# Rope on VectorE, the turns of q and k between blocks of the next projection, aligned tiles and earlier reloads of u in a hybrid S5 and attention layer

## The chip, the cores and the metric

The kernel runs on one core of a Trainium2 chip as one program. The metric is the device time in microseconds of one execution, as the median of several; a profiled execution gives the trace from which all rows below come. The engines are PE (TensorE, matmuls and transposes), ACT (ScalarE), DVE (VectorE), POOL (GpSimd) and SP (SyncE, which issues nearly all DMAs from one queue in order).

## The reference

One decoder layer, 512 positions, width 1024, one batch, float32. Cut to what matters:

```python
h = rms_norm(x, norm_w)
u_s, z_s, q, k, v, z_a, r_s, r_a = split(h @ w_in)
y_s = s5_branch(u_s, ...)                      # diagonal complex state space, GLU
y_s = (y_s * silu(z_s)) @ w_ssm_out
q, k = rms_norm(q, q_norm_w), rms_norm(k, k_norm_w)     # per head of 64
q, k = apply_partial_rope(q, pos), apply_partial_rope(k, pos)   # first 16 of 64
y_a = dilated_attention(q, k, v)               # 3 groups: window/dilation 128/1, 512/4, 2048/16
y_a = (y_a * silu(z_a)) @ w_attn_out
m = sigmoid(r_s) * y_s + sigmoid(r_a) * y_a
out = x + m @ w_o
```

There are three dilation groups (g = 0, 1, 2) of eight heads of 64 each.

## The kernel before, in words

**Projections in three products.** Each float32 operand is split into a rounded part (hi) and a rest (lo), and `mm3` (L130) makes three matmuls for each tile of 128 of the contraction: hi hi, hi lo, lo hi. A weight section of 512 KB is loaded by SP into `w_raw` (two buffers, `load_w`, L193), rounded by ACT into `w_hi` (L116) and subtracted by DVE into `w_lo` (L118), three buffers each. `plan` lists the sections in order, and `get_w` (L187) hands out the next one and starts loads two ahead. A unit (`cm_unit`, L203) is 24 matmuls of 512 columns into one bank of PSUM (`pj`).

**The order of the program.** The order in which the code names the work is only a priority. A planner places each engine's instructions by that priority among what it expects to be ready, and each engine then runs its list strictly in order. `queued()` (L69) adds a condition: PE instructions inside its block come after the PE instruction traced last.

**The u stage.** h is made and transposed (hT). Eight units `u_unit(j)` (L289) project u; each copies its bank out (uT, ACT) and stores it to a scratch in DRAM (`ud`, SP, L295), from which `load_u` (L271) reads it back in another layout: pieces of 256 bytes, into parts of `sza` for j = 0 to 3, each of which waits until the store has landed. In between, DVE makes the state-space coefficients, `w_unit` (L297) transposes them (wps, W) and `x_unit` (L313) multiplies them with the reloaded u (xps). The first three units are computed together; in the code their reloads follow `u_unit(3)` (L475 to L479).

**The middle.** Gates, the scan on DVE, the state-space output, its GLU and output projection. The change does not touch it.

**Attention, in four pairs of heads (hp).** Each pair takes two wide granules and a unit. A wide granule (`wide_granule`, L829) has four quarters kq of weights and, in each, four blocks r of 128 positions with six matmuls each: four pj banks are filled at once, and all of them are complete only in the last quarter. The first (`qk_first`, L896) gives q and k of groups 0 and 1, the second (`qk_second`, L908) q and k of group 2 and the values V of groups 1 and 2, and the unit `v0_unit` (L596) V of group 0. `qk_norm` (L846) makes the sums of squares, an inverse root by iteration, the scaling of `qraw` (DVE, L858), and then rope on POOL (L864 to L869): for each group, two products and an addition over 16 of 64 columns, four instructions. `qk_turn` (L871) transposes a group of normed q and k on PE (qtp), a = 0 for q and a = 1 for k, and ACT and DVE write hi and lo into `qkp`.

`scores` (L933) makes the scores (sps) and the softmax factors in `Pt`, which DVE scales last (L997). `values` (L1000) transposes `Pt` (ptp), copies each transposed bank to `ptb` (ACT for the first head of the pair, L1039, DVE for the second, L1041) and multiplies it with V (ot).

The banks of PSUM are dealt in turn: four for pj, three (4, 5, 6) for transposes and scores, taken in the order of the code, and the eighth for ot. V, Pt and the two qraw tiles have one buffer each.

In the loop over pairs (L1103 to L1122), while the softmax of pair hp is under way, the granules of pair hp + 1 run. The second granule calls `mid(kq)` ahead of a quarter: the turn of group 0 ahead of quarter 1, of group 1 ahead of quarter 2 (inside `queued()`), and `values(hp)` ahead of quarter 3. Then follow `v0_unit`, the turn of group 2 and the transposes of V. The last pair has no granules beside it, only units of the gate `ra`.

**Addresses.** Tiles of a pool lie one after another. In the built program of before, hT_hi and every large tile after it start 192 bytes past a multiple of 512.

Of the kernel before, what the change touches and what calls it, by code (L numbers as in the profile page):

```python
# [2 lines left out]

# [1 line left out]

# [47 lines left out]
def tile_hybrid_block(ctx: ExitStack, tc: tile.TileContext, x, positions, norm_w, w_in, lam_re, lam_im,  # L53
# [54 lines left out]
    def pj_tile():  # L108
        return ps_tile("p", "pj")
# [90 lines left out]
        split(hi, lo, raw, lo_eng=lo_w[0])  # L200
        return hi, lo

    def cm_unit(rh, rl, kts=KT):  # L203
        hi, lo = get_w()
        ps = pj_tile()
        for k in range(kts):
            mm3(ps, hi[:, k], lo[:, k], rh[:, k], rl[:, k], k == 0, k == kts - 1)
        return ps
# [5 lines left out]
    act.dma_start(nw8, norm_w[0].rearrange("(k p) -> k p", p=P))  # L214
    nwc = cst.tile([P, KT], F32, name="nwc")
    wcol = cst.tile([P, NG, 2], F32, name="wcol")
    hT_hi = cst.tile([P, KT, S], F32R, name="hT_hi")
    hT_lo = cst.tile([P, KT, S], F32R, name="hT_lo")
    nps = bank("nps")
# [51 lines left out]
    def load_u(j, Uj=None):  # L271
        if Uj is None:
            Uj = t2k("Uj")
        sp.dma_start(Uj, ud[j].rearrange("q g s c -> s q g c"))
        return Uj.rearrange("p (g c) -> p g c", g=8)
# [13 lines left out]
    def u_unit(j, ps=None):  # L289
        if ps is None:  # L290
            ps = cm_unit(hT_hi, hT_lo)
        uT = t2k("uT")

        act.copy(uT.rearrange("p (h r i j) -> p r j i h", h=2, r=4, i=NI), ps.rearrange("p (r j i h) -> p r j i h", r=4, h=2, i=NI))
        sp.dma_start(ud[j].rearrange("q g s c -> g q (s c)"), uT)  # L295
# [35 lines left out]
                mm3(ps[:, t], hi[:, k], lo[:, k], hT_hi[:, k, t], hT_lo[:, k, t], k == 0, k == KT - 1)  # L331
    for j in range(3):
        u_unit(j, first[j][1])
    lr = scr([G, N])
    li = scr([G, N])
    dt = scr([G, 1])
# [137 lines left out]

    for j in range(3, 8):  # L475
        u_unit(j)
        for i in {3: (0, 1, 2), 4: (3,)}.get(j, ()):
            early[i] = load_u(i, sza[:, i])
        wx(*((), (), (0,), (1,), (2, 3))[j - 3])  # L479


# [111 lines left out]
                            hi[:, k], lo[:, k], kh == 0 and k == 0 and rr == 0, kh == 1 and k == 3)  # L593
        return pss

    def v0_unit(hp, V):  # L596
        ps = cm_unit(hT_hi, hT_lo)
        vt = t2k("vt")
        act.copy(vt.rearrange("p (b r j) -> p r b j", r=4, b=4), ps.rearrange("p (r b j) -> p r b j", r=4, b=4))

        def finish():
            pt = bank("vtp")
            for b in range(NB):
                pe.transpose(pt[:, b * P:(b + 1) * P], vt[:, b * P:(b + 1) * P], ident)
            act.copy(V[:, 0].rearrange("p b c -> p (b c)"), pt)
        return finish
# [219 lines left out]
    if "gT" in dbg:  # L826
        sp.dma_start(dbg["gT"], gT_hi.bitcast(F32).rearrange("p k s -> p (k s)"))

    def wide_granule(th, tl, mid=None):  # L829

        pss = [pj_tile() for _ in range(NB)]
        for kq in range(4):
            if mid:
                mid(kq)
            hi, lo = get_w()
            for r in range(NB):
                for k in range(2):
                    kk = 2 * kq + k
                    mm3(pss[r], th[:, kk, r * P:(r + 1) * P], tl[:, kk, r * P:(r + 1) * P], hi[:, k], lo[:, k],
                        kk == 0, kk == KT - 1)  # L840
        return pss

    def new_raw(i):
# [2 lines left out]
    def qk_norm(gs, raws, sq):  # L846

        n = 4 * len(gs)
        v = sml.tile([P, 32], F32, name="qv", bufs=1)[:, 0:NB * n]
        rstd = sml.tile([P, 32], F32, name="qrstd", bufs=1)[:, 0:NB * n]  # L850
        qa = sml.tile([P, 32], F32, name="qa", bufs=1)[:, 0:NB * n]
        qb = sml.tile([P, 32], F32, name="qb", bufs=1)[:, 0:NB * n]
        dve.tensor_scalar(v.rearrange("p (r h) -> p r h", r=NB), sq, 1.0 / HD, EPS, op0=ALU.mult, op1=ALU.add)
        rsqrt(rstd, v, [P, NB * n], qa, qb)
        rs = rstd.rearrange("p (r h) -> p r h", r=NB)
        for i, (g, raw) in enumerate(zip(gs, raws)):
            rv = raw.rearrange("p r (h d) -> p r h d", h=4)
            dve.tensor_tensor(rv, rv, rs[:, :, 4 * i:4 * i + 4].unsqueeze(3).broadcast_to([P, NB, 4, HD]), op=ALU.mult)  # L858
            t1 = sml.tile([P, NB * 2, 2, 16], F32, name="rt1", bufs=1)
            t2 = sml.tile([P, NB * 2, 2, 16], F32, name="rt2", bufs=1)  # L860
            rh = raw.rearrange("p r (a h d) -> p (r a) h d", a=2, h=2)
            cv = tC[:, g].rearrange("p r a d -> p (r a) d").unsqueeze(2)
            sv = tS[:, g].rearrange("p r a d -> p (r a) d").unsqueeze(2)
            pool.tensor_tensor(t1, rh[:, :, :, 0:16], cv.broadcast_to([P, NB * 2, 2, 16]), op=ALU.mult)  # L864
            pool.tensor_tensor(t2[:, :, :, 0:8], rh[:, :, :, 8:16],
                               sv[:, :, :, 0:8].broadcast_to([P, NB * 2, 2, 8]), op=ALU.mult)
            pool.tensor_tensor(t2[:, :, :, 8:16], rh[:, :, :, 0:8],
                               sv[:, :, :, 8:16].broadcast_to([P, NB * 2, 2, 8]), op=ALU.mult)
            pool.tensor_tensor(rh[:, :, :, 0:16], t1, t2, op=ALU.add)  # L869

    def qk_turn(g, raw, QT, KA, KB):  # L871
        for a in range(2):
            ps = bank("qtp")
            pn = ps.rearrange("p (b r j) -> p r b j", r=4, b=4)
            for r in range(NB):
                o = pn[:, r] if g == 0 else ps[:, r * P:(r + 1) * P]
                pe.transpose(o, raw[:, r, a * P:(a + 1) * P], ident)
            if a == 0 or g == 0:
                parts = [(slice(0, P), QT[0][:, g], QT[1][:, g]) if a == 0 else (slice(0, P), KA[0], KA[1])]
            else:  # L880
                parts = [(slice(64 * h, 64 * h + 64), KB[0][64 * h:64 * h + 64, g - 1, h],
                          KB[1][64 * h:64 * h + 64, g - 1, h]) for h in range(2)]
            for sl, hi, lo in parts:
                w = wcol[sl, g, a:a + 1]
                act.activation(hi, ps[sl], AF.Copy, scale=w)  # L885
                dve.scalar_tensor_tensor(lo, ps[sl], w, hi.bitcast(F32), op0=ALU.mult, op1=ALU.subtract)  # L886
# [18 lines left out]
        qk_norm((0, 1), raws, sq)  # L905
        return raws

    def qk_second(hp, mid=None):  # L908

        pss = wide_granule(hT_hi, hT_lo, mid)  # L910
        raw = new_raw(0)
        V = new_v()
        sq = sml.tile([P, NB, 8], F32, name="ssq")[:, :, 0:4]
        for r in range(NB):
            act.copy(raw[:, r], pss[r][:, 0:256])
            squares(sq[:, r], pss[r][:, 0:256])
            act.copy(V[:, 1:3, r], pss[r][:, 256:512].rearrange("p (g c) -> p g c", g=2))  # L917
        qk_norm((2,), [raw], sq)
        return raw, V
# [80 lines left out]
    def values(hp, Pt, V):  # L1000
# [23 lines left out]
        for kind in range(2):  # L1024
            for bb in range(2):
                pts = []
                k0 = 1 if kind == 0 and bb == 0 else 0
                for h in range(2):
                    ps = bank("ptp")
                    for i in range(2):  # L1030
                        for k in range(2):
                            if 2 * i + k < k0:
                                continue
                            pe.transpose(ps[:, (2 * i + k) * P:(2 * i + k + 1) * P],
                                         Pt[:, h, kind, 2 * bb + i, k * P:(k + 1) * P], ident)
                    pt = PT[n % 4]
                    n += 1
                    if h == 0:
                        act.copy(pt[:, k0 * P:], ps[:, k0 * P:])  # L1039
# [63 lines left out]
    for hp in range(NP):  # L1103
        Pt = scores(hp, *QK)
        if hp < NP - 1:
            raws = qk_first()

            def mid(kq):
                if kq == 1:
                    qk_turn(0, raws[0], *QK)  # L1110
                if kq == 2:
                    with queued():
                        qk_turn(1, raws[1], *QK)
                if kq == 3:
                    values(hp, Pt, V)

            raw, V_next = qk_second(hp + 1, mid)
            V = V_next
            finv = v0_unit(hp + 1, V)
            qk_turn(2, raw, *QK)  # L1120
            finv()
        else:  # L1122
            for c in range(2):
                rals[c] = gate_tile()
                sp.dma_start(rals[c], rad[c])
            for c in range(n_ra + 1, KT - 2):
                ra_unit(c)
            values(hp, Pt, V)
            for c in range(KT - 2, KT):
                ra_unit(c)  # L1130
# [60 lines left out]
```

## Time and profile before

| what | value |
|---|---|
| median of 3 runs | 720.77 us (719.61 to 723.12) |
| the profiled execution's own time | 722.95 us |
| its span in the trace | 721.2 us |
| PE, PE weight loads | 689.3 us (96%), 571.6 us (79%) |
| DVE | 460.8 us (64%) |
| ACT | 314.8 us (44%) |
| POOL | 179.8 us (25%) |
| DMA, mean | 114 GB/s |

How to read it: busy times are of the whole span. PE's matmuls are pipelined and their ends are modelled, so a busy PE need not be at its peak, and a short stall can hide in a modelled end. A row of the waits gives who waited, for whom, the time in all, how often, and the longest. A row of the chain or the timeline starts with its time from the span's start and its length in us. A row of the groups gives, behind the bar, busy us, the mean ns of one, and the idle time of the engine just before, with who ended it.

### The profile page before, as it was taken

What the parts mean: (1) busy time and instruction counts of PE and PEld (TensorE: products, weight loads), DVE (VectorE), ACT (ScalarE), POOL (GpSimd) and SP (SyncE); (2) the same over time, 40 slices, a digit from 0 to 9 for tenths busy, and PEclk for the clock granted to TensorE, in tenths of its full rate; (3) what the DMA queues carried; (4) which work ended last, traced back from release to release, by engine and by line L of the source; (5) the groups of instructions that cost most, each with busy time, mean ns of one, the idle gap of its engine ahead of it and who ended that gap; (6) DMA issues with size and microseconds to landing.
All of it is one profiled execution on the core that took longest, in us unless ns stands there. A gap on an engine that the chain in (4) does not pass through costs nothing.

```text
span 721.2 us, 12599 instructions
## 1 busy us (share of the span) xinstructions
PE 689.3 (96%) x4789; PEld 571.6 (79%) x4789; DVE 460.8 (64%) x928; ACT 314.8 (44%) x631; POOL 179.8 (25%) x330
## 2 busy tenths in 40 slices
PE   2799899999999999999999999999989998999997
PEld 2697677788977888888889888788868887888886
DVE  6766865999969544674325659756764667364832
ACT  6433544423247653342144456537253734543320
POOL 3421020630316502640000326121601251220000
PEclk9989999999999999999999999999999999999999
DMA  8425742564537635555333432312312221327341
GB/s 206 107 62 149 181 108 66 131 165 153 118 86 157 150 90 161 153 163 181 104 89 100 132 88 61 87 50 69 97 50 71 77 88 30 117 75 252 128 145 59
DMA packets 137213, 82.14 MB, mean 114 GB/s; under 512 B 32696, under 2 KB 125632, under 8 KB 137024
## 3 DMA queue, kind: packets, MB, share of 16 engines
q1 hardware_dynamic: 135088, 78.96, 38.0%
q0 software_dynamic: 2048, 2.36, 2.3%
q8 instruction: 38, 0.62, 0.4%
q14 instruction: 23, 0.19, 0.1%
q10 hardware_dynamic: 16, 0.00, 0.0%
HBM read 68.46 MB, written 10.49 MB: 109 GB/s over the span
## 4 chain that ended last, share of the span: by engine, by line
PE 87%; ACT 4%; DMA 4%; SPq 2%; DVE 2%; issue 0%; ACTq 0%
PE pj L63 72%; DMA w_raw<-in_w_in_dram 4%; PE yps L63 3%; PE sps L63 3%; PE ot L63 2%; PE ptp L67 2%; PE xps L63 1%; PE kps L63 1%; ACT w_hi L116 1%; PE qtp L67 1%; SPq L454 1%; PE wps L67 1%; ACT qkp L885 1%; PE yT L67 1%; SPq L227 1%; ACT ptb L1039 1%
## 5 line engine op out<-in xcount | busy, mean ns | idle before, releaser
L116 ACT ACTIVATE w_hi<-w_raw 128x1024 fp32r<-128x1024 f32 x100 | 106.2, 1063 | 230.2 <-PE pj L63 196.7
L118 DVE TENSOR_TENSOR w_lo<-w_raw,w_hi 128x1024 fp32r<-128x1024 f32 x98 | 124.4, 1269 | 102.0 <-ACT w_hi L116 97.2
L63 PE MATMUL pj<-hT_lo,w_hi 128*128 128x512 f32 (+1 forms) x344 | 132.2, 385 | 3.6 <-DVE hT_lo L260 3.6
L63 PE MATMUL pj<-hT_hi,w_hi 128*128 128x512 f32 (+1 forms) x344 | 132.9, 389 | 2.7 <-ACT V L917 1.4
L63 PE MATMUL pj<-hT_hi,w_lo 128*128 128x512 f32 (+1 forms) x344 | 131.6, 384 | 1.6 <-DVE w_lo L118 1.6
L63 PE MATMUL pj<-w_hi,hT_hi 128*128 128x512 f32 (+1 forms) x288 | 106.5, 370 | 0.0
L63 PE MATMUL pj<-w_lo,hT_hi 128*128 128x512 f32 (+1 forms) x288 | 105.7, 367 | 0.0
L63 PE MATMUL pj<-w_hi,hT_lo 128*128 128x512 f32 (+1 forms) x288 | 105.3, 369 | 0.0
L63 PEld LDWEIGHTS pj<-hT_lo,w_hi 128*128 128x128 f32 x344 | 66.7, 194 | 16.0 <-DVE hT_lo L260 4.6
L63 PEld LDWEIGHTS pj<-hT_hi,w_hi 128*128 128x128 f32 x344 | 66.1, 193 | 15.4 <-ACT V L917 2.1
L63 PEld LDWEIGHTS pj<-hT_hi,w_lo 128*128 128x128 f32 x344 | 66.5, 193 | 14.5 <-DVE w_lo L118 2.7
L63 PEld LDWEIGHTS pj<-w_hi,hT_hi 128*128 128x128 f32 x288 | 54.4, 189 | 8.6 <-DVE Xs L651 0.2
L63 PEld LDWEIGHTS pj<-w_hi,hT_lo 128*128 128x128 f32 x288 | 54.4, 189 | 8.5
L63 PEld LDWEIGHTS pj<-w_lo,hT_hi 128*128 128x128 f32 x288 | 54.4, 189 | 8.4
L886 DVE SCALAR_TENSOR_TENSOR qkp<-qtp,wcol,qkp 128x512 fp32r<-128x512 f32 (+1 forms) x32 | 23.2, 747 | 26.9 <-ACT qkp L885 26.4
L943 ACT ACTIVATE Pt<-Pt,st 128x256 f32<-128x256 f32 (+1 forms) x64 | 31.0, 493 | 14.1 <-DVE st L941 14.0
L747 POOL TENSOR_TENSOR kt<-kt,dg 16x128 f32<-16x128 f32 x8 | 12.0, 1505 | 92.0 <-ACT kt L746 86.0
L864 POOL TENSOR_TENSOR rt<-qraw,tC 128x256 f32<-128x256 f32 x12 | 14.0, 1170 | 84.0 <-DVE qraw L858 83.7
L751 POOL DMA_DIRECT2D dd<-kt x64 | 33.7, 535 | 2.4 <-POOL kt L747 2.4
L885 ACT ACTIVATE qkp<-qtp,wcol 128x512 fp32r<-128x512 f32 (+1 forms) x32 | 21.2, 688 | 21.8 <-PE qtp L67 16.1
L973 POOL COPY sw<-st 32x4 f32<-32x4 f32 x64 | 11.9, 187 | 69.8 <-ACT Pt L943 67.0
L990 POOL COPY sfb<-sd 32x2 f32<-32x2 f32 x64 | 18.0, 282 | 27.9 <-DVE sd L986 25.1
(265 smaller groups left out, 1271.8 us busy)
## 6 DMA issues: line engine op xcount, KB each, us to landing
w_raw<-in_w_in_dram SPq DMA_DIRECT2D x40, 512.0 KB
w_raw<-in_w_in_dram SPq DMA_DIRECT2D x112, 128.0 KB
w_raw<-in_w_glu_dram SPq DMA_DIRECT2D x8, 512.0 KB
w_raw<-in_w_ssm_out_dram SPq DMA_DIRECT2D x8, 512.0 KB
w_raw<-in_w_o_dram SPq DMA_DIRECT2D x8, 512.0 KB
x_all<-in_x_dram SPq DMA_DIRECT2D x4, 512.0 KB
ud<-uT SPq DMA_DIRECT2D x8, 256.0 KB
uss<-ud SPq DMA_DIRECT2D x8, 256.0 KB
```

The source lines that it names most:

```text
L63: last[0] = nc.tensor.matmul(*a, **k)
L67: last[0] = nc.tensor.transpose(*a, **k)
L116: act.activation(hi, src, AF.Copy, scale=scale)
L118: e.tensor_tensor(lo, src, hi.bitcast(F32), op=ALU.subtract)
L747: pool.tensor_tensor(kt[:, :, T - 1, :], kt[:, :, T - 1, :], dg, op=ALU.add)
L751: pool.dma_start(M[Q * t:Q * t + Q, :, 0:P - Q * t], kt[:, :, t:].rearrange("q g k p -> q g (k p)"))
L864: pool.tensor_tensor(t1, rh[:, :, :, 0:16], cv.broadcast_to([P, NB * 2, 2, 16]), op=ALU.mult)
L885: act.activation(hi, ps[sl], AF.Copy, scale=w)
L886: dve.scalar_tensor_tensor(lo, ps[sl], w, hi.bitcast(F32), op0=ALU.mult, op1=ALU.subtract)
L943: act.activation(o, o, AF.Exp, bias=nm, scale=-1.0, accum_out=st[:, kind, 1, h, b:b + 1])
L973: pool.tensor_copy(sw[32 * r:32 * r + 32, :, :, b], st[32 * b:32 * b + 32, 1, :, :, r])
L990: pool.tensor_copy(fb[32 * b:32 * b + 32, :, r], d[32 * r:32 * r + 32, 1, :, b])
```

## The change

Six edits:

- **Rope** runs on DVE instead of POOL, the same four instructions.
- **Turns.** `qk_turn` takes which of a = 0, 1 to turn. In the second granule the four half turns stand ahead of single blocks (kq, r): (2, 3), (3, 0), (3, 1) and (3, 2). Each is inside `queued()`, and the six matmuls of its block are inside another, so that on PE they come after it. `mid` now runs after `get_w`.
- **Values** come after block (1, 3), that is ahead of the third quarter, and for pair 0 after block (2, 1). In pairs 0 to 2 ACT makes all eight copies to `ptb`; in pair 3 they stay shared.
- **v0_unit** in the loop takes one of the three banks for transposes and scores instead of a pj bank.
- **Reloads** of u for j = 0 to 2 are named right behind the three stores, ahead of `u_unit(3)`; that of j = 3 stays behind `u_unit(4)`.
- **room**, a tile of 320 bytes behind `wcol`, moves all later tiles; POOL clears one column of it.

```diff
+    room = cst.tile([P, 80], F32, name="room")
+    pool.memset(room[:, 0:1], 0.0)
...
     for j in range(3):
         u_unit(j, first[j][1])
+    for j in range(3):
+        early[j] = load_u(j, sza[:, j])
...
     for j in range(3, 8):
         u_unit(j)
-        for i in {3: (0, 1, 2), 4: (3,)}.get(j, ()):
-            early[i] = load_u(i, sza[:, i])
+        if j == 4:
+            early[3] = load_u(3, sza[:, 3])
...
-    def wide_granule(th, tl, mid=None):
+    def wide_granule(th, tl, mid=None, after=None):
...
         for kq in range(4):
-            if mid:
-                mid(kq)
             hi, lo = get_w()
             for r in range(NB):
-                for k in range(2):
-                    kk = 2 * kq + k
-                    mm3(...)
+                tied = mid(kq, r) if mid else False
+                with queued() if tied else nullcontext():
+                    for k in range(2):
+                        kk = 2 * kq + k
+                        mm3(...)
+                if after:
+                    after(kq, r)
...
-            pool.tensor_tensor(t1, rh[:, :, :, 0:16], cv.broadcast_to([P, NB * 2, 2, 16]), op=ALU.mult)
+            dve.tensor_tensor(t1, rh[:, :, :, 0:16], cv.broadcast_to([P, NB * 2, 2, 16]), op=ALU.mult)
...
-    def qk_turn(g, raw, QT, KA, KB):
-        for a in range(2):
+    def qk_turn(g, raw, QT, KA, KB, turned=(0, 1)):
+        for a in turned:
...
-                    if h == 0:
+                    if h == 0 or hp < NP - 1:
                         act.copy(pt[:, k0 * P:], ps[:, k0 * P:])
...
-            def mid(kq):
-                if kq == 1:
-                    qk_turn(0, raws[0], *QK)
-                if kq == 2:
-                    with queued():
-                        qk_turn(1, raws[1], *QK)
-                if kq == 3:
+            steps = {(2, 3): (0, 0), (3, 0): (0, 1), (3, 1): (1, 0), (3, 2): (1, 1)}
+
+            def mid(kq, r):
+                if (kq, r) not in steps:
+                    return False
+                g, a = steps[kq, r]
+                with queued():
+                    qk_turn(g, raws[g], *QK, turned=(a,))
+                return True
+
+            def after(kq, r):
+                if (kq, r) == ((2, 1) if hp == 0 else (1, 3)):
                     values(hp, Pt, V)
...
-            finv = v0_unit(hp + 1, V)
+            finv = v0_unit(hp + 1, V, bank("v0p"))
```

The other three instructions of rope change engine in the same way, and `cm_unit` and `v0_unit` get an argument for the bank.

More of the change, by code (lines that the diff above doesn't have):

```diff
@@ L1 @@
 import math
-from contextlib import ExitStack
+from contextlib import ExitStack, nullcontext
 import numpy as np
@@ L201, in load_w, with cm_unit @@
         return hi, lo
-    def cm_unit(rh, rl, kts=KT):
+    def cm_unit(rh, rl, kts=KT, ps=None):
         hi, lo = get_w()
-        ps = pj_tile()
+        if ps is None:
+            ps = pj_tile()
         for k in range(kts):
@@ L594, in tok_granule, with v0_unit @@
         return pss
-    def v0_unit(hp, V):
-        ps = cm_unit(hT_hi, hT_lo)
+    def v0_unit(hp, V, ps=None):
+        ps = cm_unit(hT_hi, hT_lo, ps=ps)
         vt = t2k("vt")
@@ L827, in tile_hybrid_block @@
         sp.dma_start(dbg["gT"], gT_hi.bitcast(F32).rearrange("p k s -> p (k s)"))
-    def wide_granule(th, tl, mid=None):
+    def wide_granule(th, tl, mid=None, after=None):
         pss = [pj_tile() for _ in range(NB)]
         for kq in range(4):
-            if mid:
-                mid(kq)
             hi, lo = get_w()
             for r in range(NB):
-                for k in range(2):
-                    kk = 2 * kq + k
-                    mm3(pss[r], th[:, kk, r * P:(r + 1) * P], tl[:, kk, r * P:(r + 1) * P], hi[:, k], lo[:, k],
-                        kk == 0, kk == KT - 1)
+                tied = mid(kq, r) if mid else False
+                with queued() if tied else nullcontext():
+                    for k in range(2):
+                        kk = 2 * kq + k
+                        mm3(pss[r], th[:, kk, r * P:(r + 1) * P], tl[:, kk, r * P:(r + 1) * P], hi[:, k], lo[:, k],
+                            kk == 0, kk == KT - 1)
+                if after:
+                    after(kq, r)
         return pss
@@ L863, in qk_norm @@
             sv = tS[:, g].rearrange("p r a d -> p (r a) d").unsqueeze(2)
-            pool.tensor_tensor(t1, rh[:, :, :, 0:16], cv.broadcast_to([P, NB * 2, 2, 16]), op=ALU.mult)
-            pool.tensor_tensor(t2[:, :, :, 0:8], rh[:, :, :, 8:16],
+            dve.tensor_tensor(t1, rh[:, :, :, 0:16], cv.broadcast_to([P, NB * 2, 2, 16]), op=ALU.mult)
+            dve.tensor_tensor(t2[:, :, :, 0:8], rh[:, :, :, 8:16],
                                sv[:, :, :, 0:8].broadcast_to([P, NB * 2, 2, 8]), op=ALU.mult)
-            pool.tensor_tensor(t2[:, :, :, 8:16], rh[:, :, :, 0:8],
+            dve.tensor_tensor(t2[:, :, :, 8:16], rh[:, :, :, 0:8],
                                sv[:, :, :, 8:16].broadcast_to([P, NB * 2, 2, 8]), op=ALU.mult)
-            pool.tensor_tensor(rh[:, :, :, 0:16], t1, t2, op=ALU.add)
-    def qk_turn(g, raw, QT, KA, KB):
-        for a in range(2):
+            dve.tensor_tensor(rh[:, :, :, 0:16], t1, t2, op=ALU.add)
+    def qk_turn(g, raw, QT, KA, KB, turned=(0, 1)):
+        for a in turned:
             ps = bank("qtp")
@@ L906, in qk_first, with qk_second @@
         return raws
-    def qk_second(hp, mid=None):
-        pss = wide_granule(hT_hi, hT_lo, mid)
+    def qk_second(hp, mid, after):
+        pss = wide_granule(hT_hi, hT_lo, mid, after)
         raw = new_raw(0)
@@ L1106, in tile_hybrid_block @@
             raws = qk_first()
-            def mid(kq):
-                if kq == 1:
-                    qk_turn(0, raws[0], *QK)
-                if kq == 2:
-                    with queued():
-                        qk_turn(1, raws[1], *QK)
-                if kq == 3:
+            steps = {(2, 3): (0, 0), (3, 0): (0, 1), (3, 1): (1, 0), (3, 2): (1, 1)}
[8 more added lines that the diff above has]
+                if (kq, r) == ((2, 1) if hp == 0 else (1, 3)):
                     values(hp, Pt, V)
-            raw, V_next = qk_second(hp + 1, mid)
+            raw, V_next = qk_second(hp + 1, mid, after)
             V = V_next
-            finv = v0_unit(hp + 1, V)
+            finv = v0_unit(hp + 1, V, bank("v0p"))
             qk_turn(2, raw, *QK)
```

## The prediction

> **What bounds the kernel now.** I read the chain of waits first, then PE's own waits, then the two places where PE waits, in time order. The page's line for the chain:
>
> ```profile
> PE 87%; ACT 4%; DMA 4%; SPq 2%; DVE 2%; issue 0%; ACTq 0%
> ```
>
> PE carries it, so only two things can shorten the kernel: less PE work (the change removes none: the same matmuls, the same transposes) or less PE idling. This is all the idling there is, in the view of PE's waits:
>
> ```profile
> PE hps L67 <- DVE x_all L248: 10.2, 1, 10.2
> PE pj L63 <- DVE hT_lo L260: 3.6, 4, 2.1
> PE ptp L67 <- ACT ptb L1039: 3.5, 6, 0.8
> PE xps L63 <- ACT W L307: 3.1, 1, 3.1
> PE nps L67 <- DMA nw<-in_norm_w_dram: 2.3, 1, 2.3
> PE pj L63 <- DVE w_lo L118: 1.6, 3, 0.8
> PE pj L63 <- ACT V L917: 1.4, 3, 0.5
> PE pj L63 <- ACT w_hi L116: 1.3, 2, 0.9
> PE ptp L67 <- DVE qkp L886: 0.6, 2, 0.3
> ```
>
> Three groups: the start (x, hT, nw: 10.2 + 3.6 + 2.3 = 16.1 us), which the diff does not touch; the u stage (xps 3.1, and part of the waits for w_lo and w_hi); and the attention pairs (ptp 3.5 + 0.6, V 1.4: 5.5 us). The whole prize is 5.5 us in attention and some 5 to 6 in the u stage.
>
> One attention pair on PE, in the timeline (start, length, and in brackets the idle time before and who ended it):
>
> ```profile
> 525.96 0.55 PE L67 MATMUL ptp<-ident,Pt 128*128 128x128 f32 x3 [0.28 <-DVE qkp L886]
> ...
> 532.07 0.66 PE L67 MATMUL ptp<-ident,Pt 128*128 128x128 f32 x4 [0.68 <-ACT ptb L1039]
> 532.66 3.00 PE L63 MATMUL ot<-ptb,V 128*64 128x128 f32 x48
> ```
>
> The values step (transposes ptp, products ot) stalls between its own transposes, and nothing fills the holes: the projection's matmuls have run out, and the next unit waits for a pj bank whose eviction V waits for ot. Yet its input was ready long before. DVE's timeline, last scaling of Pt and then the norm of q and k:
>
> ```profile
> 511.98 0.61 DVE L997 TENSOR_SCALAR Pt<-Pt,sfb 128x256 f32<-128x256 f32 x2
> ...
> 513.41 2.36 DVE L858 TENSOR_TENSOR qraw<-qraw,qrstd 128x1024 f32<-128x1024 f32 x2
> ```
>
> Pt is done at 512.59, 13 us before the step. What came late is the rope, on POOL:
>
> ```profile
> 514.81 1.56 POOL L864 TENSOR_TENSOR rt<-qraw,tC 128x256 f32<-128x256 f32 x1 [2.86 <-DVE qraw L858]
> ...
> 521.73 0.73 POOL L869 TENSOR_TENSOR qraw<-rt,rt 128x256 f32<-128x256 f32 x1
> ```
>
> Two groups took 514.81 to 522.46, 7.65 us. The turns wait for it, and values, written behind both turns and sharing three banks with them, waits for the turns. I infer that link from the order in the code; no row states it.
>
> **Rope on VectorE.** Two tensor_tensor of 256 elements and two of 128 per group, both inputs in SBUF. The nearest rows are one-pass tensor_tensor on DVE, by form:
>
> ```profile
> L858 DVE TENSOR_TENSOR qraw<-qraw,qrstd 128x1024 f32<-128x1024 f32 x9 | 10.8, 1224 | 0.4
> ...
> L126 DVE TENSOR_TENSOR qa<-qrstd 128x32 f32<-128x32 f32 x9 | 1.7, 191 | 0.2
> ```
>
> (1224 - 191) / 992 = 1.04 ns an element over 158 ns, so 425 ns and 291 ns: 1.43 us a group, 2.9 for two, against 7.65. With one w_lo between, raw is turned-ready near 513.41 + 2.36 + 2.9 + 1.2 = 519.9 instead of 522.46. DVE gets 12 groups, 17 us in all, and loses the twelve copies that go to ACT; it holds 2% of the chain. Cost on the path: 0, hidden by the matmuls between the granule's start and the first turn. If DVE were later than that, the tied turns would stop PE for the lateness, one for one.
>
> **Values ahead of the third quarter, turns between blocks.** ACT's copy row, and from the chain the pace of matmuls and the weight loads used further below:
>
> ```profile
> L1039 ACT COPY ptb<-ptp 128x512 f32<-128x512 f32 (+1 forms) x12 | 6.7, 560 | 8.4 <-PE ot L63 5.5 <-PE ptp L67 2.8
> ```
>
> ```profile
> 47.99 9.64 DMA w_raw<-in_w_in_dram
> ...
> 59.17 6.67 DMA w_raw<-in_w_in_dram
> ...
> 75.07 1.06 ACT w_hi L116
> ...
> 536.12 11.64 PE pj L63 x50
> ```
>
> A matmul of 512 costs 11.64 / 50 = 0.23 us of PE. Values now has 48 of them (11 us) behind it in pairs 1 and 2 and 36 in pair 0; the first 18 of the 48 (6 of the 36) are tied to no turn, so the planner has work to put into the holes. Eight copies on ACT instead of four are 8 x 0.56 = 4.5 us beside some 8 us of PE work of the step: covered, unless a weight split (1.06 us, the row of w_hi) falls between two copies. I leave one third of a split per pair, 1.0 us in all. Of the 3.5 + 0.6 us, 3.1 goes.
>
> The first turn now stands 30 matmuls (6.9 us) before the granule's end, which in the traced pair fell just ahead of 525.96, so near 519; but values now lies before it, some 8 us of PE (525.96 to 535.66, less its holes), so the turn comes near 525 or, where part of values slips behind it, not before 522. The rope is ready at 519.9. Margin 2 to 5 us, so the tie costs 0.
>
> The wait for V (1.4) goes whole: ot ends before the granule does, so V is free when its eviction starts, and v0 takes one of the three turn banks, whose last user was transposed three blocks earlier. What is late next is the turn of group 2, on which the scores wait; it too starts earlier, since no copies of values stand before its squares on ACT, and 24 matmuls of v0 and 96 of the next granule cover it. Attention: -3.1 - 1.4 = -4.5 us. Bounds: -5.5 (all idling gone) and 0.
>
> **Reloads of u.** SyncE's queue as it ran:
>
> ```profile
> 48.69 10.38 SPq L274 DMA_DIRECT2D sza<-ud  x3
> 59.17 2.93 SPq L197 DMA_DIRECT2D w_raw<-in_w_in_dram  x2
> ...
> 68.67 0.59 SPq L274 DMA_DIRECT2D sza<-ud  x1
> 69.36 1.23 SPq L197 DMA_DIRECT2D w_raw<-in_w_in_dram  x1
> ```
>
> The weight load of 47.99 is all that stands between the three stores of u and their reloads. The edit moves the reloads past that load and past the store of unit 3 (on SyncE alone; POOL and ACT issue none of these), and adds no wait, but the load then stands behind reloads that wait for stores to land, and behind the load stand ACT's w_hi, DVE's w_lo and PE. What PE pays in this stage today is the 3.1 us at xps, because ACT sits at w_hi until the weights of 69.36 land at 75.07, and then this:
>
> ```profile
> 79.00:82.20 3.20, 3.20 (x12) 2.49 (x9) 3.20 (x5) 2.77 (x8) 0.00 (x0) 0.50 0.73 198
> ```
>
> The third column from the end is the granted clock: 0.50 for 3.2 us after the stall, another 1.6 us lost. Together 4.7 us. If the planner keeps its order, the effect is 0. If one reload passes the weight load, that load lands perhaps 2 us later (a reload's share of 10.38 is 3.5) and the reloads end about that much sooner, and with them the store of unit 3, its reload and the load of 69.36, on which the 4.7 us hang. I take -1.0: the 0 of an unchanged order is the likeliest single value, and of the 4.7 a fifth; bounds -4.7 and +9 (rival 2).
>
> **Tiles at multiples of 512.** In the built program of before, the tiles that weights and u land in lie 192 bytes past such a multiple; room adds 320. Rows of the hardware queue in three windows: 12 to 15 us, 64-byte pieces (b); 88 to 92 us, 256-byte pieces (u); 23.9 to 25.6 us, 512-byte weight rows (the columns are packets, MB, share of 16 engines):
>
> ```profile
> q1 hardware_dynamic: 3689, 0.23, 80.4%
> q1 hardware_dynamic: 2035, 0.52, 56.9%
> q1 hardware_dynamic: 889, 0.45, 89.6%
> ```
>
> Share x window x 16 / packets: 10.5, 17.9 and 27.4 ns. The 64-byte pieces never cross a 256-byte boundary at this offset, the other two always do. Yet 7.4 ns for 192 bytes more and 9.5 for 256 more lie on one line, so crossing shows no surcharge. I take 0; the bounds are 0 and, by rival 3, -4.2. The Trainium skill, "DMA: Bandwidth & Descriptors", section "How a descriptor splits into AXI transactions", says the contrary: a descriptor that starts off a 256-byte boundary fetches from the boundary below and pays beats for the unused bytes, by which a 512-byte row at 192 would take 22 beats instead of 16, and the sum would be that of rival 3. The trace does not agree: the line through 10.5, 17.9 and 27.4 has no step. The memset of room is one small POOL instruction while POOL has no data yet: 0. Engine operands had one offset throughout, so no row shows what theirs is worth; 0.
>
> **Sum.** -4.5 (attention) - 1.0 (u) + 0 (tiles) = -5.5. The profiled execution took 722.95 with a span of 721.2, 2.2 above the median of 720.77: 717.4 on its own scale, 715.3 on the median's. A measurement of this kernel can tell about 0.5%, 3.6 us, from no change, so faster means under 717.2.
>
> **Rivals.** (1) ACT becomes the pace of values. Eight copies (4.5) and up to three splits (3.2) fill the step, and the holes stay, with a matmul only sometimes in them: the 4.1 us at ptp remain, only V's 1.4 goes, and with the u stage at 0 it ends at 719.4. For it: ACT already ended most of these waits. Against: 36 to 48 matmuls to fill with. Chance 0.22.
>
> (2) Slower: the weight load behind the reloads. All three reloads go ahead of the load of 47.99 and hold SyncE as long as now, 10.4 us; it starts near 58.4, lands after 6.67 as the one of 59.17 did, at 65.1 instead of 57.63, and PE waits 7.4 us more in front of unit 5 and runs 3.2 us at half clock, +9.0. Nothing of it comes back if the later load (69.36) is as late as now: 720.8 - 4.5 + 9.0 = 725.3. For it: an in-order queue, and reloads that need landed stores. Against: the load after it has slack, and the 4.7 us now lost at xps are then spent here and not there. It decides the sign from 8.1 us lost on. Chance 0.10.
>
> (3) Alignment pays. The line through the three packet times leaves 10.5 - 64 x 0.0385 = 8.0 ns that every packet pays whatever its size. If that is the price of the odd start, a weight row falls from 27.4 to 19.4 ns, 29%. DMA holds 4% of the chain, 29 us, mostly weight rows; half of it is waiting for a place in the queue and not transfer, so 4.2 us go: 711.1. Against it: a fixed price would not be the same for pieces that cross a boundary and pieces that don't. The Trainium skill's rule on split descriptors, above, would also end near here, at about 20 ns a row. Chance 0.10.
>
> The forecast itself, attention as worked out and the u stage within -3 to +1.5: 0.58.
>
> **Numbers.** Faster takes the forecast where the u stage does not lose (0.51) and rival 3 (0.10): 0.61. Same takes the rest of the forecast and rival 1: 0.29. Slower is rival 2: 0.10. The forecast alone spans 713 to 718; the range reaches from rival 3 (with all attention idling gone too, 710) up to 722, past rival 1, and leaves out rival 2 and little else.
>
> **What would show it.** Right: in PE's waits, ptp at 1 us or less in sum and no row for V; values in the middle of the granule in PE's timeline, ahead of the turns; rope on DVE at 0.3 to 0.45 us each; no clock slice below 0.9 near 79 if the u stage gained. Wrong: a row of PE waiting at qtp for DVE's qraw (the tie bites), ptp still at 3 us (rival 1), a gap over 5 us before the sixth u unit (rival 2), or 512-byte rows near 20 ns (rival 3). A gain over 11 us would mean that something outside these waits got faster.

## The result, and the profile after

The kernel after took 716.19 us in the median of 9 (713.54 to 719.35), the kernel before 721.1 in the median of 9 (719.61 to 723.12). The ratio is 0.9934, with a 95% interval from 0.9913 to 0.9956: 4.8 us faster, between 3.2 and 6.3. 715.3 was forecast. The profiled execution took 716.12, with a span of 714.3.

PE's waits after, all rows:

```profile
PE hps L67 <- DVE x_all L251: 10.1, 1, 10.1
PE pj L63 <- DVE hT_lo L263: 3.4, 4, 1.8
PE nps L67 <- DMA nw<-in_norm_w_dram: 2.3, 1, 2.3
PE pj L63 <- DVE w_lo L118: 1.5, 2, 1.0
PE wps L67 <- DVE ab L290: 1.0, 1, 1.0
PE xps L63 <- ACT W L310: 0.6, 1, 0.6
```

Both rows of ptp and the row of V are gone, xps fell from 3.1 to 0.6, and a wait of wps for DVE is new. So far it reads like the forecast. The same pair as in the prediction, on PE's timeline (the projection's matmuls and some repeats left out):

```profile
509.89 1.25 PE L67 MATMUL ptp<-ident,Pt 128*128 128x128 f32 x10
...
515.10 0.60 PE L67 MATMUL ptp<-ident,Pt 128*128 128x128 f32 x4
515.62 0.88 PE L63 MATMUL ot<-ptb,V 128*64 128x128 f32 x12
516.43 1.09 PE L67 MATMUL ptp<-ident,Pt 128*128 128x128 f32 x8
...
519.50 1.09 PE L63 MATMUL ot<-ptb,V 128*64 128x128 f32 x16
520.53 0.66 PE L67 MATMUL qtp<-ident,qraw 128*128 128x128 f32 x4
...
522.51 0.43 PE L63 MATMUL ot<-ptb,V 128*64 128x128 f32 x2
522.87 0.66 PE L67 MATMUL qtp<-ident,qraw 128*128 128x128 f32 x4
523.46 1.09 PE L63 MATMUL ot<-ptb,V 128*64 128x128 f32 x14
```

In before it started here:

```profile
525.19 0.49 PE L67 MATMUL ptp<-ident,Pt 128*128 128x128 f32 x3
```

Values starts at 509.89 instead of 525.19, ahead of the turns, and no bracket shows a wait. But PE now goes back and forth between transposes, products and projection. What that costs, the waits don't show. So I laid the two traces beside each other: both have 4789 PE instructions; each was given the usual distance to the next start for its form, and the lead is the difference in time at which both kernels had done the same amount of that work (worked out from the starts of all PE records; minus is ahead of before):

```
us in before:    30    50    70    92   400 | 430   475   545   615   670
after          -0.7  -2.1  -2.0  -6.0  -5.9 |-6.0  -3.4  -5.3  -7.1  -6.8
```

Of the lead, 5.9 us are there at 400 us, before attention begins. From there on pair 0 loses 2.5, pairs 1 and 2 gain 1.8 and 1.9, the last pair loses 0.3: attention, from which 4.5 was expected, gives 0.9. And of the lead at 92 us, 2.1 is there at 50, before the first reload can have done anything. Most of that is the granted clock behind the wait for hT, which the trace has at 0.50 for 3.4 us after and for 6.8 before: 1.7 us lost more (third column from the end; after, then before):

```profile
34.70:37.90 3.20, 3.20 (x15) 3.20 (x16) 3.20 (x17) 0.06 (x1) 0.00 (x0) 0.50 0.00 0
37.90:41.40 3.50, 3.50 (x31) 3.50 (x31) 2.47 (x9) 1.01 (x2) 0.00 (x0) 1.00 0.00 0
```

```profile
34.70:37.90 3.20, 2.38 (x11) 2.27 (x11) 3.20 (x15) 0.92 (x2) 0.37 (x1) 0.50 0.00 0
37.90:41.40 3.50, 3.50 (x19) 3.50 (x18) 3.41 (x15) 0.00 (x0) 0.00 (x0) 0.50 0.00 0
```

With the stretch at 0.50 from 79 us on, which before has and after has not, the clock makes 3.4 of the 6.0 us at 92 us. Nothing in the diff but the addresses touches the stage of hT, and one profile can't say whether they did it. Hence the experiments: each part alone, and each part undone.

### The profile page after: what moved, and what is told of

It reads as the page before. It is cut to its first block, busy times and chain, and to the rows that moved or that the text cites. A ratio compares the mean times of both kernels' runs of the same rounds, so it can differ in the third digit from the quotient of the medians.

```text
span 714.3 us, 12582 instructions
## 1 busy us (share of the span) xinstructions
PE 691.0 (97%) x4789; PEld 570.9 (80%) x4789; DVE 461.6 (65%) x964; ACT 320.6 (45%) x643; POOL 136.6 (19%) x283
## 4 chain that ended last, share of the span: by engine, by line
PE 90%; DMA 3%; SPq 2%; DVE 2%; ACT 2%; issue 1%; POOL 0%; ACTq 0%
PE pj L63 71%; PE sps L63 3%; PE yps L63 3%; DMA w_raw<-in_w_in_dram 3%; PE ot L63 2%; PE v0p L63 2%; PE ptp L67 2%; PE qtp L67 2%; PE xps L63 1%; PE kps L63 1%; SPq L459 1%; PE wps L67 1%; PE yT L67 1%; SPq L230 1%; ACT w_hi L116 1%
## 5 line engine op out<-in xcount | busy, mean ns | idle before, releaser
L118 DVE TENSOR_TENSOR w_lo<-w_raw,w_hi 128x1024 fp32r<-128x1024 f32 x98 | 121.1, 1236 | 93.2 <-ACT w_hi L116 92.8
L63 PE MATMUL pj<-hT_lo,w_hi 128*128 128x512 f32 (+1 forms) x320 | 121.4, 380 | 3.4 <-DVE hT_lo L263 3.4
L63 PE MATMUL pj<-hT_hi,w_hi 128*128 128x512 f32 (+1 forms) x320 | 122.3, 385 | 0.1
L63 PE MATMUL pj<-hT_hi,w_lo 128*128 128x512 f32 (+1 forms) x320 | 120.9, 379 | 1.5 <-DVE w_lo L118 1.5
L63 PEld LDWEIGHTS pj<-hT_lo,w_hi 128*128 128x128 f32 x320 | 61.0, 191 | 14.6 <-DVE hT_lo L263 4.4
L63 PEld LDWEIGHTS pj<-hT_hi,w_lo 128*128 128x128 f32 x320 | 61.0, 190 | 13.0 <-DVE w_lo L118 2.2
L63 PEld LDWEIGHTS pj<-hT_hi,w_hi 128*128 128x128 f32 x320 | 60.7, 191 | 11.3 <-ACT w_hi L116 0.6
L63 PEld LDWEIGHTS sps<-qkp 128*128 128x128 f32 (+1 forms) x192 | 23.2, 187 | 4.3 <-issue 1.6
L63 PE MATMUL sps<-qkp 128*128 128x256 f32 (+2 forms) x192 | 25.6, 287 | 0.0
```

Of the source, the lines that this page charges most:

```text
L63: last[0] = nc.tensor.matmul(*a, **k)
L118: e.tensor_tensor(lo, src, hi.bitcast(F32), op=ALU.subtract)
```

## Experiments

All ratios are to the kernel before, measured beside it on the same chip.

**Each part alone.** Before with the tile:

```diff
+    room = cst.tile([P, 80], F32, name="room")
+    pool.memset(room[:, 0:1], 0.0)
```

> The kernel before with the tile of 320 bytes alone. Theory A (alignment is worth nothing; the 2.1 us by which the changed kernel leads at 45 us come from the shorter stretch at half clock behind the hT stall): within 1 us of the before of these rounds, packets of 512 bytes near 28 ns as at the old offset, and the time spread follows the mean granted clock. Theory B (alignment is what made the start shorter): 2 us faster, and the stretch at clock 0.50 behind the hT stall is short (3.2 us, not 6.6) in the profile.

Measured: 720.35 against 722.49, ratio 0.9969 (0.9951 to 0.9987), 2.2 us faster. Theory A falls. B named the size but not the cause: the mean granted clock was 0.9928, no better than 0.9932 of before in the same rounds.

Before with the reloads:

```diff
+    for j in range(3):
+        early[j] = load_u(j, sza[:, j])
...
-        for i in {3: (0, 1, 2), 4: (3,)}.get(j, ()):
-            early[i] = load_u(i, sza[:, i])
+        if j == 4:
+            early[3] = load_u(3, sza[:, 3])
```

> The kernel before with the reloads of u behind their stores alone. Theory A (the traces after the result): one reload ahead of the weight load, the PE wait at xps falls from 3.1 us to 0.6 or 0.7, and the stretch at clock 0.50 near 79 us goes: 3 to 5 us faster, about 717. Theory B (the prediction as it stood): 1 us faster, 720. Theory C (the changed queue has cost elsewhere in the u stage): no faster than before.

Measured: 0.9982 (0.9962 to 1.0002), 1.3 us faster and not quite apart from nothing. A's 3 to 5 us fell; those were read off one pair of profiles. PE's waits in this kernel:

```profile
PE xps L63 <- ACT W L307: 1.7, 1, 1.7
PE wps L67 <- DVE ab L287: 1.5, 1, 1.5
```

The wait at xps is shorter by 1.4, and a wait for DVE's coefficients, which before did not have, takes 1.5.

Before with the three attention edits, that is the change without these two:

```diff
-    room = cst.tile([P, 80], F32, name="room")
-    pool.memset(room[:, 0:1], 0.0)
...
-    for j in range(3):
-        early[j] = load_u(j, sza[:, j])
...
-        if j == 4:
-            early[3] = load_u(3, sza[:, 3])
+        for i in {3: (0, 1, 2), 4: (3,)}.get(j, ()):
+            early[i] = load_u(i, sza[:, i])
```

> The kernel before with the three attention edits (rope on DVE, half turns, values earlier with ACT's copies and the bank for v0), without reloads and room. Theory A (the traces after the result): pairs 1 and 2 gain 1.9 us each, pair 0 loses 2.5 us because PE changes 15 times more between products, transposes and projection, the last pair loses 0.3: in sum 0.5 to 1.0 us faster, about 720.3. Theory B (the prediction as it stood): 4.5 us faster, 716.6.

Measured: 0.9983 (0.9968 to 0.9998), 1.2 us faster; in the trace the lead changes from 400 us on by +2.5, -1.9, -1.9 and +0.3 over the pairs, -1.0 in sum. Theory A holds. PE's order is that of the changed kernel, and so is the result to 0.1 us. Yet this kernel's profile led before's by 2.3 us at 92 us, where nothing in it was edited: so much may one profile of the first 92 us be off. The clock alone more than accounts for it, since before's profile lost 5.1 us to it up to there and this one 1.7.

The three parts alone add up to 4.7 us, the change gave 4.8. Each part is known to 1.1 to 1.4 us either way only, so the agreement to 0.1 is partly chance. Over all timed executions the granted clock took (one less the mean clock, times the time) about 5.0 us of before and 2.7 of after, so 2.3 of the 4.8 us came back through the clock. In the kernels with one part it took 5.2 (tile), 3.5 (reloads) and 4.3 (attention): the tile's gain is not the clock's, and all that the reloads gain alone can be.

**Addresses, the other way round.** The changed kernel without the tile, and with one of 64 bytes:

```diff
-    room = cst.tile([P, 80], F32, name="room")
+    room = cst.tile([P, 16], F32, name="room")
```

> The changed kernel without the tile of 320 bytes, so that its large tiles lie 192 bytes past a multiple of 512 again; PE's order is the same. Theory A (the odd start lengthens some packets, 28.6 instead of 28.1 ns in the mean for 512 bytes with the same median, which costs about 2.5 us in the first 92 us): 2 to 3 us slower than the changed kernel, near 0.9965 of before, with the mean packet back at 28.6 ns. Theory B (the 2.2 us of the kernel before with the tile alone were chance): within 0.7 us of the changed kernel, near 0.9935 of before.

> The changed kernel with a tile of 64 bytes in place of 320: large tiles lie at 256 past a multiple of 512, that is on a 256-byte boundary and not on a 512-byte one. If the 256-byte boundary counts: as the changed kernel, near 0.9935 of before, mean 512-byte packet 28.1 ns. If the 512-byte boundary counts: as without the tile, 2 to 3 us slower, mean 28.6 ns.

Measured: 0.9963 (0.9949 to 0.9978) without, 0.9927 (0.9903 to 0.9950) with 64 bytes. Taking the tile away costs 2.1 us of the 4.8, and an offset of 256 does as well as 512: the boundary that counts is 256. The page's rows of the hardware queue (packets, MB, share of 16 engines over the span), without the tile, with 64 bytes, and in the kernel after:

```profile
q1 hardware_dynamic: 135088, 78.96, 38.5%
```

```profile
q1 hardware_dynamic: 135088, 78.96, 37.5%
```

```profile
q1 hardware_dynamic: 135088, 78.96, 37.8%
```

Share x span x 16 / packets gives 32.8, 31.8 and 32.0 ns a packet (spans 718.3, 716.8, 714.3). All profiles sort the same way: 32.5 to 32.8 ns in the four kernels at 192, 31.6 to 32.0 in the ten at a multiple of 256. From the single packet records, by size:

```
             192 past, before and 3 others   multiple of 256, 10 kernels
256 bytes    median 18, mean 18.9 to 20.1    median 18, mean 18.0
512 bytes    median 27, mean 28.5 to 28.7    median 27, mean 28.0 to 28.2
```

The usual packet costs the same at either offset. What the odd start lengthens is a minority: 7 to 13% of the 256-byte packets took over 1.3 times the median at 192, 0.1 to 0.6% at a multiple of 256. Time and long packets go with the offset alike; that these packets are what costs the 2.1 us is not shown. The work of the engines on the moved tiles is not it: w_hi took 1063 ns a piece in before and with the tile alone, w_lo 1269 and 1270.

**Rope.** The changed kernel with rope on POOL again:

```diff
-            dve.tensor_tensor(t1, rh[:, :, :, 0:16], cv.broadcast_to([P, NB * 2, 2, 16]), op=ALU.mult)
+            pool.tensor_tensor(t1, rh[:, :, :, 0:16], cv.broadcast_to([P, NB * 2, 2, 16]), op=ALU.mult)
...
-            dve.tensor_tensor(rh[:, :, :, 0:16], t1, t2, op=ALU.add)
+            pool.tensor_tensor(rh[:, :, :, 0:16], t1, t2, op=ALU.add)
```

> The changed kernel with rope back on POOL. Theory A (rope is not what delays, now that values stand ahead of the turns: the margin from rope to the first turn is 4.4 us in the traced pair, rope on POOL takes 4.7 us longer for two groups, and the second group's turn comes 5.4 us behind the first): within 0.7 us of the changed kernel, 716 to 717. Theory B (the prediction's mechanism: a late rope stops PE at the tied turns for the lateness, 4.7 less 4.4 at least and all of 4.7 where the margin is gone, three times): 2 us or more slower than the changed kernel, 718 to 724, with PE rows that wait at qtp for POOL's qraw.

Measured: 0.9953 (0.9935 to 0.9970), 1.4 us slower than the changed kernel, with intervals that overlap, and neither theory: there is no wait for POOL's qraw, and pair 0 loses only 0.1, pairs 1 and 2 gain 2.0 and 2.2. All is lost in the last pair, 4.6 us, where PE reaches values at 642.01, before Pt is scaled (DVE's last row of it, and PE's wait):

```profile
646.01 0.61 DVE L1004 TENSOR_SCALAR Pt<-Pt,sfb 128x256 f32<-128x256 f32 x2 [0.31 <-POOL sfb L997]
```

```profile
PE ot L63 <- DVE ptb L1048: 1.9, 1, 1.9
```

Of the 4.6 us, 1.7 are a stretch of 3.4 us at clock 0.50 that begins at 646.83, during that wait. There the planner gave values 19 projection matmuls behind the scores instead of 39. To test that, the same kernel with one gate unit more ahead of the last values:

```diff
-            for c in range(n_ra + 1, KT - 2):
+            for c in range(n_ra + 1, KT - 1):
                 ra_unit(c)
             values(hp, Pt, V)
-            for c in range(KT - 2, KT):
+            for c in range(KT - 1, KT):
                 ra_unit(c)
```

> The changed kernel with rope on POOL and one more gate unit ahead of the last pair's values. Theory A (with values ahead of the turns, rope on POOL is not late; in the trace of rope on POOL the pairs 0 to 2 gain 4.1 us against before, 3.2 more than in the changed kernel, and all of its loss, 4.5 us, lies in the last pair, where PE reaches values before Pt is scaled): 3 to 3.5 us faster than the changed kernel, near 0.989 of before, about 713. Theory B (rope on POOL delays the turns): no faster than the changed kernel.

Measured: 714.62, ratio 0.9898 (0.9875 to 0.9921), 2.6 us faster than the changed kernel; attention is 2.9 us ahead of before. Theory A holds, a little below its 3 to 3.5: with values ahead of the turns, rope on POOL delays nothing. Pair 0 of this kernel on PE:

```profile
446.18 1.72 PE L67 MATMUL ptp<-ident,Pt 128*128 128x128 f32 x14
447.83 0.43 PE L63 MATMUL ot<-ptb,V 128*64 128x128 f32 x2
448.19 0.66 PE L67 MATMUL ptp<-ident,Pt 128*128 128x128 f32 x4
448.78 0.87 PE L63 MATMUL ot<-ptb,V 128*64 128x128 f32 x10
...
451.68 0.60 PE L67 MATMUL qtp<-ident,qraw 128*128 128x128 f32 x4
```

From 428 to 475 us (of before) PE changes the kind of its work (tile written and shape) 25 times in before, 32 times here and 40 times in the changed kernel, and the same instructions take 46.9, 47.1 and 49.5 us. In the changed kernel's pair 0 the sums of starts say where: products +0.63, transposes +0.45, scores +0.82, turns +0.21, projection with v0 +0.41. Nothing of that is a wait in the view of PE's waits. V's wait of 0.5 us at the end of the pair is gone in both, so 7 more changes took 0.7 us here and 15 more took 3.0 there: 0.1 to 0.2 us each on average. That is a division and no price of every change. Around single changes in the attention of all 14 traces (starts against the usual distances, medians) going from products to projection takes 0.25 us, from scores to projection and from products to transposes 0.1, and from projection to transposes or back 0.02 or less. And the 0.82 of the scores comes with shorter runs of them: twelve of one shape took 1.25 us in before, two runs of six took 0.90 each in the changed kernel.

**The pieces of the attention edit.** The changed kernel with values behind the last block, with shared copies, and with v0 in a projection bank, one at a time:

```diff
-                if (kq, r) == ((2, 1) if hp == 0 else (1, 3)):
+                if (kq, r) == (3, 3):
```

> The changed kernel with values named behind the last block of the granule, that is behind all four half turns, as in before, with rope on DVE, ACT's copies and the bank for v0 kept. Theory A (the place of values is what fills the holes between its transposes): PE waits at ptp for ACT of 2 us or more in sum come back, and from 400 us on the kernel is 2 to 4 us slower than the changed one. Theory B (early rope and ACT's copies do it, whatever the place): ptp waits of 1 us or less, within 1 us of the changed kernel.

```diff
-                    if h == 0 or hp < NP - 1:
+                    if h == 0:
```

> The changed kernel with the copies of transposed Pt shared between ACT and DVE in all pairs, as in before. Theory A (the place of values fills the holes, and who copies is worth nothing): ptp waits 1 us or less, from 400 us on within 1 us of the changed kernel. Theory B (a copy on DVE stands behind norm, rope and weight splits): PE waits at ptp or ot for DVE's ptb of 2 us or more in sum, 1 to 3 us slower.

```diff
-            finv = v0_unit(hp + 1, V, bank("v0p"))
+            finv = v0_unit(hp + 1, V, None)
```

> The changed kernel with v0 in a bank of the projection again. Theory A (V is free early because its products end before the granule does): no PE wait for V, within 0.7 us of the changed kernel. Theory B (without a bank of its own v0 waits for the eviction of a pj bank): PE waits at pj for ACT's V of 0.4 us a pair, 1.2 us in sum, and the kernel is about 1 us slower.

Values late: 1.0080 (1.0057 to 1.0103), 10 us slower than the changed kernel. Its waits:

```profile
PE ptp L67 <- ACT ptb L1046: 5.9, 3, 2.0
...
PE ot L63 <- DVE ptb L1048: 1.9, 1, 1.9
```

Theory A, and more than it named: with half turns and values this late the kernel is slower than before. Two things enlarge it. The place is later than in before, which named values ahead of the last 24 matmuls of the granule. And by the trace 3.0 us are lost in the last pair, which the edit does not touch but where the planner again put only 19 matmuls behind the scores, and 1.6 in a stretch at clock 0.50 from 595.65 on, behind one of the ptp waits. Some 4.9 us are left for the place itself. Shared copies: 0.9952 (0.9932 to 0.9973), 1.3 us slower than the changed kernel, with intervals that overlap; by the trace 1.4 are lost in pair 0 and 0.4 gained in pair 1, with one wait of ot for DVE, in pair 0:

```profile
PE ot L63 <- DVE ptb L1048: 1.9, 1, 1.9
```

That is B's wait in one pair only. v0 in a projection bank: 714.60, ratio 0.9887 (0.9865 to 0.9909), as fast as rope on POOL with one gate unit more, with attention 2.6 us ahead of before instead of 0.9. No wait for V appears, so theory A is right about V, but neither theory saw that the bank costs something. The last scores of pair 1, in this kernel and then in the changed one:

```profile
496.92 1.20 PE L63 MATMUL sps<-qkp 64*128 64x256 f32 x12
```

```profile
496.86 0.97 PE L63 MATMUL sps<-qkp 64*128 64x256 f32 x6
498.19 0.98 PE L63 MATMUL sps<-qkp 64*128 64x256 f32 x6
```

With a bank taken from the three for transposes and scores, the planner splits these scores in two with projection between: 2.30 us from start to start instead of 1.62 for all 18 of this form in the pair, 0.7 of the 0.85 us that a pair gains without the bank. That holds for pairs 1 and 2; in pair 0 the scores are split with either bank, and whole, as in before, only with rope on POOL.

**The lead over the pairs,** from the same comparison of starts (us against before, minus is a gain):

```
                             pair 0   pair 1   pair 2   last   sum
changed kernel                 +2.5     -1.8     -1.9   +0.3   -0.9
rope on POOL                   +0.1     -2.0     -2.2   +4.6   +0.5
... and a gate unit more       +0.1     -2.0     -2.2   +1.2   -2.9
values late                    +3.2     +0.3     +1.8   +3.3   +8.6
shared copies                  +3.9     -2.2     -1.9   +0.3   +0.1
v0 in a projection bank        +2.5     -2.7     -2.7   +0.3   -2.6
```

The low clock is in these numbers: 1.7 of the 4.6 in the last pair of rope on POOL, and 1.6 of the 1.8 in pair 2 of values late. Rope on POOL, one gate unit more and v0 in a projection bank together were not tried.

**Reloads and the clock.** The changed kernel with the reloads where they were:

> The changed kernel with the reloads of u where they were, behind unit 3; PE's order is the same. Theory A (the reloads shorten PE's wait at xps, and with it a stretch of 3.4 us at clock 0.50 that follows a wait of 3 us goes more often than not): mean granted clock 0.994 instead of 0.996, xps wait of 2 us or more, 1 to 2 us slower than the changed kernel, near 0.995 of before. Theory B (the reloads are worth nothing): same clock and time as the changed kernel, near 0.993.

Measured: 0.9935 (0.9915 to 0.9956), no slower than the changed kernel, though the mean granted clock is 0.9938 instead of 0.9962 and PE's waits and clock are what A expects:

```profile
PE xps L63 <- ACT W L310: 3.6, 1, 3.6
```

```profile
71.50:78.00 6.50, 5.31 (x40) 4.38 (x41) 6.50 (x12) 5.18 (x11) 0.00 (x0) 0.51 0.58 149
```

Alone the reloads gave 1.3 us, undone they cost nothing; what they are worth lies between 0 and some 1.5 us, and these intervals don't settle it.

Last, the changed kernel with work for PE in the wait for hT:

```diff
+    warm = psum.tile([P, 512], F32, name="warm", tag="b%d" % deal["g"][(dealt["g"] + 1) % len(deal["g"])])
+    with queued():
+        for _ in range(16):
+            pe.transpose(warm[:, 0:P], ident, ident)
```

> The changed kernel with 16 transposes of the identity, which nothing reads, on PE behind the second batch of transposes of h, that is in the wait for hT_lo near 31 us (extra work, output unchanged). Theory A (the stretch at clock 0.50 from 34.7 us on follows from PE standing still for 2 us before it): the stretch goes, the mean clock rises from 0.996 to 0.998 or more, 1.5 us faster than the changed kernel. Theory B (the stretch comes from something else, or the transposes delay the work behind them): same clock, 0 to 1.5 us slower.

Measured: 716.17, ratio 0.9921 (0.9902 to 0.9940), not to be told from the changed kernel. Its profile has no stretch of low clock near 35 us, but neither have those of four kernels without the extra work (attention alone, values late, shared copies, v0 in a projection bank), so theory A is not settled. It has one from 60 us on, behind a new wait, since the order of the u units shifted:

```profile
PE pj L63 <- ACT uT L301: 3.4, 1, 3.4
```

```profile
60.00:64.00 4.00, 4.00 (x13) 3.10 (x11) 2.60 (x7) 0.43 (x1) 0.00 (x0) 0.57 0.63 150
```

## Why the prediction was right, and where it was wrong

The time was right to 0.9 us, and the sum was right for a poor reason: -4.5 for attention measured -1.2 alone, 0 for the tiles measured -2.2, -1.0 for the reloads measured -1.3 alone and nothing when undone. That 3.3 us too much in attention and 2.2 too little at the tiles nearly cancel is luck.

- **What bounds the kernel: right.** PE carries 90% of the chain after, and its work stayed the same. But 2.3 of the 4.8 us came back as granted clock, which the forecast had only as a share of 1.6 us in the u stage.
- **Values earlier, -3.1: the waits went, the time did not.** The forecast left 1.0 us at ptp; nothing is left. In pair 1 the sums of starts give -2.8 for transposes and -0.3 for products (V's wait of 0.5 among the latter, less new changes), but +0.6 for scores, +0.6 for projection with v0, +0.1 for turns: 1.8 gained. In pair 0, whose holes were already partly filled with projection, there was little to gain and 2.5 went to the more broken order. The step that failed is "the planner has work to put into the holes": it priced the holes and let the filling be free. The place of values itself was rightly found: behind the whole granule values cost some 4.9 us more in pairs 0 to 2.
- **V, -1.4, and v0's bank.** V's wait went because ot ends before the granule does, as argued. The bank that I counted for it was not needed and costs 1.7 us in the trace; "v0 takes one of the three turn banks" looked at when that bank comes free and not at the scores that rotate through the same three.
- **Rope on DVE: cost right, link wrong.** The groups by line after:

```profile
L871 DVE TENSOR_TENSOR rt<-qraw,tC 128x256 f32<-128x256 f32 x12 | 5.1, 421 | 0.1
L872 DVE TENSOR_TENSOR rt<-qraw,tS 128x128 f32<-128x128 f32 x12 | 3.4, 285 | 0.0
```

  421 and 285 ns against 425 and 291 forecast. In the pair above the first turn starts at 520.53, and DVE's timeline has the end of rope at 515.75 + 0.43 = 516.18, a margin of 4.4 within the 2 to 5 forecast:

```profile
513.57 0.42 DVE L871 TENSOR_TENSOR rt<-qraw,tC 128x256 f32<-128x256 f32 x1
...
515.75 0.43 DVE L876 TENSOR_TENSOR qraw<-rt,rt 128x256 f32<-128x256 f32 x1
```

  But that rope was what held values up, the link inferred from the code, can matter only while values stand behind the turns. No run moves rope alone, so the link stays not shown, and with rope early and values late the waits at ptp were not shorter (5.9 us). Once values are ahead, rope on POOL is as good, and better for the order that the planner then finds.
- **Copies on ACT: right.** They are covered: no wait for ACT's copies is left. What sharing them costs, 1.0 us by the trace, is within the noise of the times. Rival 1 had ptp's 4.1 us remain; none remains.
- **Reloads: right in kind.** One reload passes the weight load and one new wait stands against the shorter one. SyncE's queue after:

```profile
42.49 3.33 SPq L298 DMA_DIRECT2D ud<-uT  x3
46.52 0.60 SPq L277 DMA_DIRECT2D sza<-ud  x1
47.23 3.98 SPq L197 DMA_DIRECT2D w_raw<-in_w_in_dram  x1
51.31 4.39 SPq L277 DMA_DIRECT2D sza<-ud  x2
```

  Rival 2, all three reloads ahead of the load, did not happen: no u unit waits 5 us. The 3.9 us that the pair of profiles shows between 50 and 92 us, 1.7 of them the clock, is more than either timing of the edit bears out.
- **Tiles, 0: wrong.** "Crossing shows no surcharge" came from a line through three windows whose means (17.9 and 27.4 ns) lie at the usual packet (medians 18 and 27). The usual packet has none indeed; a tail of longer ones comes with the offset, and so do 2.2 us of the 4.8. Rival 3 had the sign but not the mechanism: 512-byte rows did not fall to 19.4 ns; their median stayed at 27. The rule of the Trainium skill ("DMA: Bandwidth & Descriptors", "How a descriptor splits into AXI transactions") named the right boundary, 256, and deserved more than I gave it, though the surcharge of 6 beats on each row, estimated from it in the prediction, shows in no run. Where in the first 92 us the 2.2 us are gained is open; from 100 to 400 us the lead is flat to 0.1 us in every kernel but the one with extra transposes.

## What to carry to other kernels

A wait that goes is time gained only less what fills it: work cut into shorter runs lost 0.1 to 0.2 us for each further change here, which no view of waits shows, so compare the starts of equal work before believing an emptied list of waits. Before a bank or a place in the order is moved, look at who else rotates through it. And where a stage varies by 2 us from one execution to the next, a pair of profiles proves nothing there: time each part alone and each part undone.

## What the runs showed of the hardware that I had not expected

- **The clock after a wait.** Low stretches of the granted clock last 3.4 us at 0.50, each losing 1.7 us, or two such lengths in a row; the profiles had none to three each. In the u stage they follow the wait at xps: in the seven profiles where PE waited there 2.3 us or more (2.3, 2.3, 2.9, 3.1, 3.5, 3.6, 4.1) the clock fell to 0.50 within 2 us of the end of that wait, in the seven with 1.7 us or less it did not. Behind the waits for hT_lo, the longest of which took 0.9 to 2.1 us, it fell in some profiles and not in others, and in three profiles it fell at 26 to 27 us behind two waits for weights of 0.5 to 1.0 us each. The traces show a grid: within a profile the stretches begin whole multiples of 3.413 us apart (34.56 and 78.94 in before, 13 of them). Of the steps of this grid at full clock between 18 and 705 us, all six in which PE was busy for less than 42% were followed by the low clock, 13 of 26 with 45 to 57%, and none with more (modelled busy times of PE's records). So what a wait of 2 us costs depends on how it falls on the grid. The loss is also a large part of the scatter between executions: with it taken off each, the standard deviation of the nine of after falls from 1.8 to 1.1 us. The Trainium skill ("TensorE: Matmul & The Clock Gate", "What's actually happening") has a clock that follows how busy PE was, by a free-running window of 3.4 us; the lengths of 3.4 us agree. Its rule to leave no idle gap above 3.4 us ("HAM oscillation — how this bites in real kernels") is too wide for this kernel: waits of 2.3 and 2.9 us were enough.
- **Addresses.** Tiles that start 192 bytes past a multiple of 256, the only odd offset tried, leave the usual DMA packet as it is and lengthen a minority: 32.5 to 32.8 ns in the mean of all packets against 31.6 to 32.0.
